# Sample states decayed ahead of their corrections, with four smaller moves in the queues, in a fused decoder layer

## The chip, the cores and the metric

The kernel runs on one core of one Trainium2 chip. The metric is the device time of one execution in microseconds (us), of which several runs are taken. The core has five engines with a queue of instructions each, which each engine works through in order: PE (TensorE, matmuls), ACT (ScalarE), DVE (VectorE), POOL (GpSimd) and SP (SyncE, which here issues most DMAs). POOL can issue DMAs as well. Instructions wait on semaphores for what other engines or DMAs have to have done.

## The reference

One layer of a hybrid decoder, for a prompt of 1024 tokens (x 1024 channels) and for 8 sample sequences of one token each, with shared weights, all in fp32. Cut to what matters:

```
h   = rmsnorm(x) * (1 + scale1) + shift1
qkv, gate, beta, a, sq, sk, sv, ga, gb = split(h @ w_in)
y_a = gated_rmsnorm(gated_delta_rule(conv4(qkv))) @ w_gdn_out     # 8 heads, 128 x 128 state each
y_b = sliding_window_attention(sq, sk, sv) @ w_swa_out
x   = x + gate1 * ((sigmoid(ga) * y_a + sigmoid(gb) * y_b) @ w_o)
h2  = rmsnorm(x) * (1 + scale2) + shift2
x   = x + gate2 * ((silu(conv3(h2 @ w_ffn_gate)) * (h2 @ w_ffn_up)) @ w_ffn_down)
y   = rmsnorm(x)
```

For a sample, the delta rule is one step on the state S of each head and sequence, which is an output too:

```
S     = S * exp(g)                                  # decay
delta = (v - k @ S) * beta
S     = S + outer(k, delta)                         # correction
o     = q @ S
```

## The kernel before

Matmuls of fp32 accuracy are made of three: each operand x is split into a high part (`wh`, `b1h`, ..., an ACT copy to a short format, L129) and a low part (`wl`, `b1l`, ..., a DVE subtraction, L130), and PE adds high x high (L180), high x low and low x high (L181, L182). `load_w` loads a weight tile of 1024 x 128 into `raw` (SP, L135) and splits it. In the stage of the two output projections w_swa_out and w_gdn_out there is one `raw` buffer, so that the load of the next tile is issued only when the low part of the one before has been made. Tokens come in blocks of 384, 384 and 264 columns, the last with the 8 samples.

The sample part is `sample_delta`, a generator whose pieces are woven among the matmuls of the output projections. The 64 sample states of 128 x 128 (8 heads x 8 sequences) lie in SBUF, three heads to a tile, in tiles named `b1h`, `b1l` and again `b1h`. 128 matmuls read them (L1172); copies (L1176) and a transpose bring the products k @ S and q @ S into columns; `delta` is computed in columns, transposed and written to DRAM as `dlr` (L1194). For each head SP loads its row of `dlr` spread over all 128 partitions (L1214, 512 KB written, into one of two rooms named `b1l`). Then ACT scales each 128 x 128 piece of it by k (L1216, 64 times), DVE makes S * egb + that piece in one instruction (L1217, 64 times; `egb` holds exp(g)), and POOL issues the store of the head's states (L1219). Between these, the root of the output's norm runs on POOL (`power`, L125), and its result leads to the sample columns (`osm`) of the operand of w_gdn_out.

Then comes w_o (`output_pass`, in four quarters q of the columns, 256 or 260 each), whose weights `output_weights(j)` loads (L1448) and splits. Its outputs x are squared and summed over channels for the second norm: ones-matmuls on PE (L1496), scale on DVE (`rs`, L1501), power -1/2 on POOL (L125), diagonal matrix on DVE (`dg`, L1505), spread by PE (L1506). The first FFN tile pair (`pair_weights`, `pair_product`) uses sums and differences of quarters of the operands and weights, a fast matrix product of seven terms: `ws` are weight sums on POOL (L1589), `minus` are differences of operands on DVE (L1538), `X` the operands, `pk` and `bmh`/`bml` some of their parts. The last norm, of q = 3, runs while the first FFN products of the left half have begun.

The order of each queue comes from the tile framework, which schedules by priorities. `weave` gives the pieces of several generators priorities from a start and a step, `later(f, by)` shifts those of one piece, and `issue_after(x)` holds the instructions within it behind instruction x in the planning.

Of the kernel before, what the change touches and what calls it, by code (L numbers as in the profile page):

```python
# [12 lines left out]
AF = mybir.ActivationFunctionType  # L13
ALU = mybir.AluOpType
# [4 lines left out]
P = 128  # L19
NP = 1024  # L20
NS = 8
NT = NP + NS
KC = 8
H = 8
# [40 lines left out]
class Step:  # L65
# [56 lines left out]

    def power(self, out, in_, expo):
        e = expo[:in_.shape[0], :]
        self.nc.gpsimd.tensor_tensor(out, in_, e.broadcast_to(list(in_.shape)), op=ALU.pow)  # L125

    def split(self, hi, lo, x, eng=None):

# [992 lines left out]
    def sample_delta(self, pool2):  # L1121

        nc, I = self.nc, self.I
        zl, cw = self.zl, self.cw
        S0, load = self.S0, self.load_state
        small = carver(*(self.flat_room(pool2, "b2", x, 2) for x in "hl"))
        act, tmp = small(24, NS), small(24, NS)
        nc.vector.tensor_tensor(act, zl[:, 3:11, :].rearrange("p b c -> p c b"), bc(cw[:, 3, :], 2, NS), op=ALU.mult)
        nc.vector.tensor_tensor(act, act, self.gsp, op=ALU.add)
        nc.scalar.activation(tmp, act, AF.Tanh, scale=0.5)  # L1130
        nc.vector.scalar_tensor_tensor(act, tmp, 1.0, act, op0=ALU.add, op1=ALU.mult)

        flat = lambda a: a.rearrange("p a h b -> p (a h b)")
        f3 = lambda a: a.rearrange("p h b -> p (h b)")
        qk = act[:, 0:16, :].rearrange("p (a h) b -> p a h b", a=2)
        v = act[:, 16:24, :]
        sq = small(2, H, NS)
        nc.vector.tensor_tensor(sq, qk, qk, op=ALU.mult)
        wide = small(H, NS, 2 * NS)
        nc.gpsimd.memset(wide, 0.0)  # L1140
        yield
        c, db = (self.flat_room(self.b1, "b1", x, 2) for x in "hl")
        load(6, c)
        load(7, c)
        ps = self.t(self.psm, [P, 1], "mm")
        nc.tensor.matmul(ps, flat(sq), self.ones[:, 0:1], start=True, stop=True)
        r = self.rows_rsqrt(small, ps, P, 1.0, 4 * EPS)
        yield
        rl = self.rows_spread(*r).rearrange("p (a h b) -> p a h b", a=2, h=H)
        kq = self.const([P, H, NS, 2], "kq")  # L1150
        nc.vector.tensor_tensor(kq[:, :, :, 0], qk[:, 1], rl[:, 1], op=ALU.mult)
        nc.vector.scalar_tensor_tensor(kq[:, :, :, 1], qk[:, 0], P ** -0.5, rl[:, 0], op0=ALU.mult, op1=ALU.mult)
        for i in range(2):
            nc.vector.tensor_copy(wide.rearrange("p h b c -> p h (b c)")[:, :, i::2 * NS + 2], kq[:, :, :, i])
        yield
        pr = small(H, NS)
        nc.vector.tensor_tensor(pr, kq[:, :, :, 0], kq[:, :, :, 1], op=ALU.mult)
        dots = self.t(self.psm, [P, H, NS], "mm")
        nc.tensor.matmul(f3(dots), self.ones, f3(pr), start=True, stop=True)
        qkd = small(H, NS)  # L1160
        nc.vector.tensor_copy(qkd, dots)
        yield
        eg = self.egb[:, :, 0, :].rearrange("p b h -> p h b")
        beta = self.egb[:, :, 1, :].rearrange("p b h -> p h b")

        rows = small(2, P, r=1)
        nc.gpsimd.memset(rows, 0.0)
        for i in range(2):
            ps = self.t(self.psm, [P, P], "mm")
            for b in range(NS):  # L1170
                for h in range(4):
                    nc.tensor.matmul(ps[32 * h:32 * h + 2 * NS], wide[:, 4 * i + h, b, :], S0[4 * i + h][:, b, :],  # L1172
                                     start=b == 0, stop=b == NS - 1)
            for h in range(4):
                at = slice(32 * h, 32 * h + 2 * NS)
                (nc.scalar.copy if h % 2 else nc.vector.tensor_copy)(rows[at, i, :], ps[at])  # L1176
            yield
        pks = self.t(self.psm, [P, 2 * P], "mm")
        for i in range(2):
            self.transpose(pks[:, i * P:(i + 1) * P], rows[:, i, :])  # L1180
        pks = pks.rearrange("p (h c) -> p h c", c=32)[:, :, :2 * NS].rearrange("p h (b a) -> p h b a", a=2)
        yield
        pk, dl, o = small(H, NS, 2), small(H, NS), small(H, NS)
        nc.vector.tensor_tensor(pk, pks, bc(eg, 3, 2), op=ALU.mult)
        nc.vector.tensor_scalar_mul(dl, v, 0.5)
        nc.vector.tensor_tensor(dl, dl, pk[:, :, :, 0], op=ALU.subtract)
        nc.vector.tensor_tensor(dl, dl, beta, op=ALU.mult)
        yield
        ps = self.t(self.psm, [H * NS, P], "mm")
        self.transpose(ps, f3(dl))  # L1190
        dlT = small(P, r=1)[:H * NS]
        nc.vector.tensor_copy(dlT, ps)
        dlr = self.t(self.dr, [H, NS, P], "dlr")
        nc.sync.dma_start(dlr.rearrange("h b v -> (h b) v"), dlT)  # L1194
        yield
        nc.vector.tensor_tensor(o, qkd, dl, op=ALU.mult)
        nc.vector.tensor_tensor(o, o, pk[:, :, :, 1], op=ALU.add)

        nc.vector.tensor_tensor(pr, o, o, op=ALU.mult)
        yield  # L1200
        ps = self.t(self.psm, [H * NS, 1], "mm")
        nc.tensor.matmul(ps, f3(pr), self.ones[:, 0:1], start=True, stop=True)
        r = self.rows_rsqrt(small, ps, H * NS, 1.0 / P, EPS)
        yield
        rl = self.rows_spread(*r).rearrange("p (h b) -> p h b", h=H)
        nc.vector.tensor_tensor(o, o, rl, op=ALU.mult)
        self.osm = self.const([P, H, NS], "osm")
        nc.vector.scalar_tensor_tensor(self.osm, o, self.onw, self.sgs, op0=ALU.mult, op1=ALU.mult)

        for h in range(H):  # L1210
            if h % 4 == 0:
                yield
            d = db[:, h % 2 * NP:h % 2 * NP + NP].rearrange("p (b v) -> p b v", b=NS)
            nc.sync.dma_start(d, dlr[h].unsqueeze(0).broadcast_to([P, NS, P]))  # L1214
            for b in range(NS):
                nc.scalar.activation(d[:, b, :], d[:, b, :], AF.Copy, scale=kq[:, h, b, 0:1])  # L1216
                nc.vector.scalar_tensor_tensor(S0[h][:, b, :], S0[h][:, b, :], self.egb[:, b, 0, h:h + 1], d[:, b, :],  # L1217
                                               op0=ALU.mult, op1=ALU.add)
            nc.gpsimd.dma_start(self.O[3][0][:, h].rearrange("b k v -> k b v"), S0[h])  # L1219

    def rows_rsqrt(self, small, ps, n, scale, eps):

# [180 lines left out]
    def room(self, tag, shape):  # L1403
        pool = self.bm if tag[0] == "b" else self.pk if int(tag[2]) < 4 else self.pk2
        return self.t(pool, shape, tag, F32R)

    def output_pass(self, pool, q):

        nc = self.nc
# [3 lines left out]
        def add(t, ps):  # L1413
            self.add_gated(t, ps, j, 16)
            sq = self.t(pool, [P, QW], "nsq" if j else "nss", bufs=2)[:, :n]
            if q == 3 and j > 4:
                nc.vector.tensor_tensor(sq, x1[:, j, :], x1[:, j, :], op=ALU.mult)
            else:
                nc.scalar.activation(sq, x1[:, j, :], AF.Square)
            if j == 0:  # L1420
# [5 lines left out]
                self.squares[q].append(sq)  # L1426

        for j in range(8):
            if q == 0:
                self.wo.append(self.output_weights(j))  # L1430
            nc.sync.dma_start(x1[:, j, :], self.xT[j][:, lo:lo + n])
            if q or j:
# [46 lines left out]
    def second_norm(self, pool, psum, t):  # L1479

        nc = self.nc
# [17 lines left out]
        for w, c0, c1 in ((P, 0, 2), (n - 2 * P, 2, nc_)):  # L1499
            if c0 < c1:  # L1500
                nc.vector.tensor_scalar(rs[:w, c0:c1], ss[:w, c0:c1], 1.0 / NP, EPS, op0=ALU.mult, op1=ALU.add)  # L1501
        self.power(rs[:, :nc_], rs[:, :nc_], self.mhalf)
        yield
        dg = self.t(pool, [P, 3, P], "dg", bufs=1)[:, :nc_]
        nc.vector.tensor_tensor(dg, bc(self.ident, 1, nc_), bc(rs[:, :nc_], 2, P), op=ALU.mult)  # L1505
# [15 lines left out]
    def operands(self, pool, p, stage):  # L1521
# [13 lines left out]
            yield  # L1535
            return
        d = self.t(pool, [P, 4, QW], "td", bufs=1)[:, :, :n]
        minus = lambda out, x, y: self.nc.vector.tensor_tensor(out, x, y, op=ALU.subtract)  # L1538
        minus(a1, b1, a1)
        self.split(*ops[3], a1)  # L1540
        yield
        minus(d, b2, a1)
        self.split(*ops[2], d)
        yield
        minus(b1, b2, b1)
        self.split(*ops[4], b1)
        yield
        minus(a2, a2, d)
# [104 lines left out]
    def ffn_gate_up(self, pool, pool2, psum, f, w, first):  # L1653
# [36 lines left out]

        if first:
            ss, r = self.norm_at
            self.pair_product(psum, w, (0,), gate, {2: ss, 4: r})
        self.pair_product(psum, w, (1,) if first else (0, 1), gate)
        w = self.pair_weights(pool, I["w_ffn_up"][0], f, nc.vector if first else None)

        def up(p, i, q, ps, r):
# [206 lines left out]
    def second_half(self):  # L1904

        nc, S = self.nc, ExitStack
        with S() as c:
# [6 lines left out]
            with S() as right:  # L1914
                xr = self.pool("xr", 1, ctx=right, side="right")
                with S() as left:
                    xl = self.pool("xl", 1, ctx=left)
                    self.x1 = [self.t(pl, [P, KC, n], "x1") for pl, (_, n) in zip((xl, xr), HALF)]
                    self.x1d = self.t(self.dr, [KC, P, NT], "x1d")
                    self.squares, self.X, self.wo = {}, {}, []  # L1920
                    norm = lambda q: self.second_norm(xr, psum, q)
                    self.weave((chain(*(self.output_pass(xr, q) for q in range(4))), 0, 1),
                               (self.ffn_states(xr, psum), 460, 30),
# [2 lines left out]
                               (chain(norm(2), self.operands(xr, 1, 0)), 730, 120))  # L1926
                with S() as left:
                    pool = self.pool("pf", 1, ctx=left)
                    w = self.pair_weights(pool, self.I["w_ffn_gate"][0], 0)
                    last, ops = norm(3), self.operands(xr, 1, 1)  # L1930
                    self.weave((chain(islice(last, 3), islice(ops, 1), last, ops), -100, 1))
                    right.close()
# [139 lines left out]
```

## Time and profile before

| what | value |
|---|---|
| median of 3 runs | 2085.34 us |
| lowest and highest | 2084.30 and 2087.26 us |
| profiled execution, span of its instructions | 2084.4 us |
| mean granted TensorE clock in it | 0.991 |
| PE busy | 2012.7 us, 97% |
| DVE, ACT, POOL busy | 65%, 43%, 25% |

The page gives the profiled execution as its span, with no second time; the median of the runs stands 0.9 us above that span. A row of the trace gives a start in us from the span's beginning, a length in us, the engine, the line, what is written and read, and in brackets for how long the engine stood idle before it and what ended that. A view of windows gives for each stretch its length, the busy time of PE, PE's weight loads, DVE, ACT and POOL with the number of instructions, the granted clock, the DMA share and GB/s.

### The profile page before, as it was taken

Reading aid. Unit: us, or ns where it says so; the run is one execution under the profiler, and the core shown is the slowest. Engines: PE = TensorE matmul, PEld = TensorE weight load, DVE = VectorE, ACT = ScalarE, POOL = GpSimd, SP = SyncE. Lnnn points to the kernel's source line nnn. Section 1 sums busy time; section 2 is a strip of 40 time slices with the busy share of each in tenths; the row PEclk is TensorE's granted clock in tenths of the full one; section 3 lists DMA queues with packets and bytes.
Section 4 is the critical chain, followed back from the end, with each engine's and each line's share of the span. In section 5 each row is a group of like instructions: output and inputs, shape, how many; then the busy total and the mean of one; then the engine's idle time right before and its main releaser. Section 6 shows DMA issues by size and latency. Waiting matters only on the chain.

```text
span 2084.4 us, 41297 instructions
## 1 busy us (share of the span) xinstructions
PE 2012.7 (97%) x16245; PEld 1910.2 (92%) x16245; DVE 1347.8 (65%) x2714; ACT 900.2 (43%) x2233; POOL 520.2 (25%) x594
## 2 busy tenths in 40 slices
PE   7999998999999999989989999999999999999897
PEld 4987877799999999989989999999999999999897
DVE  5755768473655647656544675578876776767756
ACT  4664545433344243432342542354444444534443
POOL 2000000121321221201111000005575466446421
PEclk9999999999999999999999999999999999999999
DMA  8256443331332322312275855323333333488862
GB/s 300 62 144 210 135 167 116 117 94 51 80 80 61 73 72 52 89 42 62 63 223 172 285 186 163 112 63 97 105 91 112 102 92 112 136 305 266 291 215 94
DMA packets 301887, 275.75 MB, mean 132 GB/s; under 512 B 59730, under 2 KB 248111, under 8 KB 301676
## 3 DMA queue, kind: packets, MB, share of 16 engines
q1 hardware_dynamic: 295642, 252.14, 39.6%
q0 software_dynamic: 5552, 20.37, 2.8%
q8 instruction: 127, 2.08, 0.4%
q14 instruction: 68, 0.56, 0.1%
q10 hardware_dynamic: 498, 0.61, 0.1%
HBM read 212.93 MB, written 62.51 MB: 132 GB/s over the span
## 4 chain that ended last, share of the span: by engine, by line
PE 83%; DVE 5%; DMA 5%; ACT 3%; issue 1%; SPq 1%; POOL 1%; DVEq 0%; POOLq 0%; ACTq 0%
PE mm L180 19%; PE mm L181 18%; PE mm L182 18%; PE wv L180 3%; PE wv L182 3%; PE wv L181 3%; PE wy L182 2%; PE wy L180 2%; PE wy L181 2%; PE pv L652 1%; PE pt L190 1%; PE tp L190 1%; DVE x L1472 1%; PE mm L264 1%; PE rc L954 1%
## 5 line engine op out<-in xcount | busy, mean ns | idle before, releaser
L180 PE MATMUL mm<-b1h,wh 128*128 128x384 f32 (+1 forms) x1520 | 496.9, 328 | 3.7 <-ACT gt L1294 1.6
L181 PE MATMUL mm<-b1l,wh 128*128 128x384 f32 (+1 forms) x1520 | 489.3, 323 | 0.0
L182 PE MATMUL mm<-b1h,wl 128*128 128x384 f32 (+1 forms) x1520 | 488.0, 323 | 0.3 <-DVE wl L130 0.3
L180 PEld LDWEIGHTS mm<-b1h,wh 128*128 128x128 f32 x1520 | 286.7, 189 | 12.4 <-issue 4.6
L181 PEld LDWEIGHTS mm<-b1l,wh 128*128 128x128 f32 x1520 | 287.1, 189 | 4.4 <-issue 3.1
L182 PEld LDWEIGHTS mm<-b1h,wl 128*128 128x128 f32 x1520 | 286.3, 189 | 3.9 <-issue 2.8
L129 ACT ACTIVATE wh<-raw 128x1024 fp32r<-128x1024 f32 x83 | 87.0, 1049 | 122.4 <-PE mm L181 70.2
L130 DVE TENSOR_TENSOR wl<-raw,wh 128x1024 fp32r<-128x1024 f32 x82 | 101.0, 1233 | 57.2 <-ACT wh L129 55.1
L181 PE MATMUL mm<-pk,w 128*128 128x260 f32 (+1 forms) x440 | 124.8, 284 | 1.1 <-DVE pk L130 1.1
L180 PE MATMUL mm<-pk,w 128*128 128x260 f32 (+1 forms) x440 | 124.8, 284 | 0.0
L182 PE MATMUL mm<-pk,w 128*128 128x260 f32 (+1 forms) x440 | 124.5, 283 | 0.0
L130 DVE TENSOR_TENSOR w<-ws,w 128x512 fp32r<-128x512 f32 x88 | 78.0, 886 | 36.9 <-ACT w L129 36.7
L1626 ACT COPY bml<-mm 128x256 f32<-128x256 f32 (+1 forms) x132 | 48.9, 371 | 100.6 <-PE mm L182 96.7
L180 PE MATMUL mm<-bmh,w 128*128 128x260 f32 (+1 forms) x320 | 90.3, 282 | 0.0
L182 PE MATMUL mm<-bmh,w 128*128 128x260 f32 (+1 forms) x320 | 90.1, 282 | 0.0
L1681 DVE SCALAR_TENSOR_TENSOR fa<-fz,fcw,fa 128x512 f32<-128x512 f32 x88 | 75.2, 874 | 18.2 <-ACT fa L1679 17.9
L180 PE MATMUL mm<-b2h,wh 128*128 128x384 f32 (+1 forms) x256 | 83.2, 328 | 2.9 <-ACT wh L129 2.8
L181 PEld LDWEIGHTS mm<-pk,w 128*128 128x128 f32 x440 | 83.2, 189 | 1.3 <-DVE pk L130 1.3
L181 PE MATMUL mm<-b2l,wh 128*128 128x384 f32 (+1 forms) x256 | 83.6, 327 | 0.4 <-DVE b2l L130 0.4
L180 PEld LDWEIGHTS mm<-pk,w 128*128 128x128 f32 x440 | 83.2, 189 | 0.2 <-ACT bml L1626 0.2
L182 PEld LDWEIGHTS mm<-pk,w 128*128 128x128 f32 x440 | 83.4, 190 | 0.0
L182 PE MATMUL mm<-b2h,wl 128*128 128x384 f32 (+1 forms) x256 | 82.8, 326 | 0.0
(645 smaller groups left out, 5886.2 us busy)
## 6 DMA issues: line engine op xcount, KB each, us to landing
raw<-in_w_in_dram SPq DMA_DIRECT2D x59, 512.0 KB
ws<-in_w_ffn_down_dram SPq DMA_DIRECT2D x55, 256.0 KB
raw<-xd SPq DMA_DIRECT2D x47, 258.0 KB
raw<-in_w_ffn_down_dram SPq DMA_DIRECT2D x47, 256.0 KB
raw<-in_w_ffn_gate_dram SPq DMA_DIRECT2D x22, 512.0 KB
raw<-in_w_ffn_up_dram SPq DMA_DIRECT2D x22, 512.0 KB
qst<-in_w_mod_dram SPq DMA_DIRECT2D x16, 512.0 KB
raw<-in_w_mod_dram SPq DMA_DIRECT2D x16, 512.0 KB
```

Source lines behind the costliest of these rows:

```text
L129: self.nc.scalar.activation(hi, x, AF.Copy)
L130: (eng or self.nc.vector).tensor_tensor(lo, x, hi.bitcast(F32), op=ALU.subtract)
L180: mm(ps, whi, xhi, start=first, stop=False, **kw)
L181: mm(ps, whi, xlo, start=False, stop=False, **kw)
L182: self.last_mm = mm(ps, wlo, xhi, start=False, stop=last, **kw).ins
L190: self.nc.tensor.transpose(out, in_, self.ident[:p, :p])
L264: nc.tensor.matmul(ps[32 * j:32 * j + 32], self.cT[:, k0 + j, :], ws[j // 2][:, j % 2, :], start=k0 == 0, stop=k0 > 0)
L652: nc.tensor.matmul(pv[64 * r:64 * r + 64], V[:, n - back, ch], ps[:, r::2, :], start=back == 0, stop=back == (n > 0))
L954: yield step(nc.tensor.matmul(ds, kd[:, n, :], s, start=True, stop=True))
L1472: nc.vector.scalar_tensor_tensor(x[:, :np_], ps[:, :np_], by[:, j, 8:9], x[:, :np_], op0=ALU.mult, op1=ALU.add)
L1626: self.last_copy = nc.scalar.copy(r[p, i], x[p])
L1681: nc.vector.scalar_tensor_tensor(ai[:, c:e], zi[:, j + c:j + e], col(j), ai[:, c:e], op0=ALU.mult, op1=ALU.add)
```

## The change

1. `decay_states` multiplies the 64 states by `egb` in place, on ACT (L1236), in pieces from the matmuls that read them on. The scaling of the spread rows on ACT is gone: DVE's instruction is now d * k + S (L1225). The spread rows go by POOL's queue (L1216 of the changed kernel), two at the start and each later one behind the store (L1227) of the head two before.
2. `output_weights` for j < 3 is called ahead of the weaving with `later(..., -150)`, no longer in `output_pass`.
3. The first root of the second norm goes on record (`first_root`), and the weights of the first FFN tile are held behind it.
4. The first product of the left half (pair 0) is held behind the last square (`last_square`), and the first products of pair 1 behind the last norm's sums (`ss`).
5. In pair 1 the difference `minus(b1, b2, b1)` goes to POOL.

```diff
+        decay = self.decay_states()
+        next(decay)
         pks = self.t(self.psm, [P, 2 * P], "mm")
 ...
-        yield
+        next(decay)
+        yield
+        next(decay)
         pk, dl, o = small(H, NS, 2), small(H, NS), small(H, NS)
 ...
         yield
+        next(decay)
         ps = self.t(self.psm, [H * NS, P], "mm")
 ...
+        room = lambda h: db[:, h % 2 * NP:h % 2 * NP + NP].rearrange("p (b v) -> p b v", b=NS)
+        spread = lambda h: nc.gpsimd.dma_start(room(h), dlr[h].unsqueeze(0).broadcast_to([P, NS, P]))
+        yield
+        spread(0)
+        spread(1)
         for h in range(H):
-            if h % 4 == 0:
+            if h == 4:
                 yield
-            d = db[:, h % 2 * NP:h % 2 * NP + NP].rearrange("p (b v) -> p b v", b=NS)
-            nc.sync.dma_start(d, dlr[h].unsqueeze(0).broadcast_to([P, NS, P]))
+            d = room(h)
             for b in range(NS):
-                nc.scalar.activation(d[:, b, :], d[:, b, :], AF.Copy, scale=kq[:, h, b, 0:1])
-                nc.vector.scalar_tensor_tensor(S0[h][:, b, :], S0[h][:, b, :], self.egb[:, b, 0, h:h + 1], d[:, b, :],
+                nc.vector.scalar_tensor_tensor(S0[h][:, b, :], d[:, b, :], kq[:, h, b, 0:1], S0[h][:, b, :],
                                                op0=ALU.mult, op1=ALU.add)
             nc.gpsimd.dma_start(self.O[3][0][:, h].rearrange("b k v -> k b v"), S0[h])
+            if h + 2 < H:
+                spread(h + 2)
+
+    def decay_states(self):
+
+        for h in range(H):
+            for b in range(NS):
+                s = self.S0[h][:, b, :]
+                self.nc.scalar.activation(s, s, AF.Copy, scale=self.egb[:, b, 0, h:h + 1])
+            if h % 2:
+                yield
 ...
-            if q == 0:
+            if q == 0 and j > 2:
                 self.wo.append(self.output_weights(j))
 ...
-        self.power(rs[:, :nc_], rs[:, :nc_], self.mhalf)
+        root = self.power(rs[:, :nc_], rs[:, :nc_], self.mhalf)
+        if t == 0:
+            self.first_root = root
 ...
-        minus(b1, b2, b1)
+        minus(b1, b2, b1, self.nc.gpsimd if p else self.nc.vector)
 ...
-            self.pair_product(psum, w, (0,), gate, {2: ss, 4: r})
-        self.pair_product(psum, w, (1,) if first else (0, 1), gate)
+            with self.tc.issue_after(self.last_square.ins):
+                self.pair_product(psum, w, (0,), gate, {2: ss, 4: r})
+        self.pair_product(psum, w, (1,) if first else (0, 1), gate, {0: ss, 1: ss} if first else {})
 ...
+                    for j in range(3):
+                        self.wo.append(self.later(lambda: self.output_weights(j), -150))
 ...
-                    w = self.pair_weights(pool, self.I["w_ffn_gate"][0], 0)
+                    with self.tc.issue_after(self.first_root.ins):
+                        w = self.pair_weights(pool, self.I["w_ffn_gate"][0], 0)
```

On ACT, in the stage of w_swa_out, before (`wh` are high parts of weight tiles; the row of `wh_12807` begins at 1139.33 in the trace, that of `wh_12982` at 1153.48 and that of `wh_13019` at 1159.58):

```order
L129 ACTIVATE wh_12807<-raw_12805 128x1024
L1176 COPY b2l_2048_12698<-mm_12850 16x128 x2
L129 ACTIVATE wh_12845<-raw_12843 128x1024
L1176 COPY b2l_2048_12698<-mm_12915 16x128 x2
L129 ACTIVATE wh_12982<-raw_12980 128x1024
L1106 COPY z_13039<-mm_13040 96x256
L1107 COPY z_13039<-mm_13040 72x128
L129 ACTIVATE wh_13019<-raw_13017 128x1024
```

The same place now; twenty more rows L1236 stand between `wh_12807` and the first one shown:

```order
L1176 COPY b2l_2048_12698<-mm_12850 16x128
L1236 ACTIVATE b1h_1875_11803<-b1h_1875_11803,egb 128x128 x5
L129 ACTIVATE wh_12845<-raw_12843 128x1024
L1236 ACTIVATE b1h_1875_11803<-b1h_1875_11803,egb 128x128 x3
L1236 ACTIVATE b1l_1876_11804<-b1l_1876_11804,egb 128x128 x5
L1176 COPY b2l_2048_12698<-mm_12850 16x128
L1236 ACTIVATE b1l_1876_11804<-b1l_1876_11804,egb 128x128 x5
L1176 COPY b2l_2048_12698<-mm_12915 16x128
L1236 ACTIVATE b1l_1876_11804<-b1l_1876_11804,egb 128x128 x10
L1236 ACTIVATE b1h_2051_12733<-b1h_2051_12733,egb 128x128 x2
L129 ACTIVATE wh_12982<-raw_12980 128x1024
```

So 50 decays, three copies and one other split now stand between the splits `wh_12807` and `wh_12982`; the other 14 stand between `wh_12982` and the next split.

On POOL, at the start of the FFN, before (`rs` are the roots of the second norm by quarters, `ws` the weight sums of the first FFN tile):

```order
L1393 DMA sgx_14296<-sga_2614 128x264
L1589 TENSOR_TENSOR ws_15523<-raw_15513,raw_15515 128x512
L1589 TENSOR_TENSOR ws_15525<-ws_15523,raw_15513 128x512
L1589 TENSOR_TENSOR ws_15533<-raw_15513 128x512
L125 TENSOR_TENSOR rs_15396<-rs_15396,mhalf 128x2
L125 TENSOR_TENSOR rs_15431<-rs_15431,mhalf 128x2
```

and now:

```order
L1412 DMA sgx_14296<-sga_2614 128x264
L125 TENSOR_TENSOR rs_15396<-rs_15396,mhalf 128x2
L1610 TENSOR_TENSOR ws_15523<-raw_15513,raw_15515 128x512
L1610 TENSOR_TENSOR ws_15525<-ws_15523,raw_15513 128x512
L1610 TENSOR_TENSOR ws_15533<-raw_15513 128x512
L125 TENSOR_TENSOR rs_15431<-rs_15431,mhalf 128x2
```

The first root has moved ahead of the three weight sums. On ACT around the first split of w_o (`w_14338`, high part) the rows before are

```order
L129 ACTIVATE bmh_2117_13460<-t_2040_12684 128x4
L129 ACTIVATE bmh_2119_13462<-t_2040_12684 128x260
L129 ACTIVATE w_2200_14338<-raw_14336 128x512 x2
L129 ACTIVATE pk_2205_14376<-raw_14374 128x1024
L129 ACTIVATE w_2209_14412<-raw_14410 128x1024
```

and now

```order
L129 ACTIVATE bmh_2117_13460<-t_2040_12684 128x4
L129 ACTIVATE bmh_2119_13462<-t_2040_12684 128x260
L129 ACTIVATE w_2200_14338<-raw_14336 128x512 x2
L129 ACTIVATE pk_2203_14346<-raw_14344 128x1024
L129 ACTIVATE w_2205_14351<-raw_14349 128x1024
```

Only numbers of tiles differ.

More of the change, by code (lines that the diff above doesn't have):

```diff
@@ L124, in power @@
         e = expo[:in_.shape[0], :]
-        self.nc.gpsimd.tensor_tensor(out, in_, e.broadcast_to(list(in_.shape)), op=ALU.pow)
+        return self.nc.gpsimd.tensor_tensor(out, in_, e.broadcast_to(list(in_.shape)), op=ALU.pow)
     def split(self, hi, lo, x, eng=None):
@@ L1416, in add @@
             if q == 3 and j > 4:
[L1417 removed]
+                self.last_square = nc.vector.tensor_tensor(sq, x1[:, j, :], x1[:, j, :], op=ALU.mult)
             else:
@@ L1537, in operands @@
         d = self.t(pool, [P, 4, QW], "td", bufs=1)[:, :, :n]
-        minus = lambda out, x, y: self.nc.vector.tensor_tensor(out, x, y, op=ALU.subtract)
+        minus = lambda out, x, y, eng=self.nc.vector: eng.tensor_tensor(out, x, y, op=ALU.subtract)
         minus(a1, b1, a1)
```

## The prediction

> **What bounds the kernel now.** I read the page first (span, busy shares, chain of waits), then PE's waits in the stretch in which the change moves instructions, then the granted clock there, then the queues one by one.
>
> ```profile
> span 2084.4 us, 41297 instructions
> ...
> PE 2012.7 (97%) x16245; PEld 1910.2 (92%) x16245; DVE 1347.8 (65%) x2714; ACT 900.2 (43%) x2233; POOL 520.2 (25%) x594
> ...
> PE 83%; DVE 5%; DMA 5%; ACT 3%; issue 1%; SPq 1%; POOL 1%; DVEq 0%; POOLq 0%; ACTq 0%
> ```
>
> PE is busy for 97% of the span and carries 83% of the chain. The change takes no matmul away, so it can only gain or lose where PE stands still, or runs at half clock. PE's waits from 1140 to 1430 us, the whole stretch that the change touches (for what, total, times, longest):
>
> ```profile
> PE mm L180 <- ACT wh L129: 2.8, 1, 2.8
> PE mm L1439 <- ACT w L129: 2.1, 1, 2.1
> PE nr L1506 <- DVE dg L1505: 1.6, 1, 1.6
> PE wv L180 <- ACT w L129: 1.1, 1, 1.1
> PE mm L181 <- DVE pk L130: 1.1, 1, 1.1
> PE mm L182 <- DVE pk L130: 0.8, 1, 0.8
> PE wv L181 <- DVE pk L130: 0.3, 1, 0.3
> ```
>
> I call them A (2.8, a w_gdn_out tile at 1192), B (2.1, the first w_o tile at 1282), E (0.8, at 1302), D (1.6, the first root of the second norm, at 1321) and C (0.3, 1.1 and 1.1 at 1405 to 1410, the last norm's operands). That is 9.8 us in all, less than 0.5% of the span. The clock adds to it. Where I cut the trace into pieces of 3.41 us (PE busy is the second figure, the granted clock stands behind POOL's):
>
> ```profile
> 888.30:891.71 3.41, 1.64 (x68) 1.31 (x68) 3.30 (x4) 0.37 (x1) 0.00 (x0) 1.00 0.51 149
> 1086.28:1089.69 3.41, 1.67 (x10) 1.28 (x10) 2.48 (x3) 2.21 (x3) 0.00 (x0) 1.00 0.72 238
> 1192.09:1195.50 3.41, 0.58 (x4) 0.48 (x4) 3.08 (x10) 3.41 (x9) 0.53 (x1) 1.00 1.05 390
> 1195.50:1198.91 3.41, 3.41 (x17) 3.41 (x16) 3.41 (x6) 2.29 (x4) 0.35 (x1) 0.50 1.06 400
> 1280.84:1284.25 3.41, 1.60 (x14) 1.39 (x12) 1.82 (x6) 1.03 (x4) 0.00 (x0) 1.00 0.21 46
> 1407.13:1410.54 3.41, 1.22 (x8) 0.81 (x7) 3.41 (x5) 1.44 (x2) 0.00 (x0) 1.00 0.00 0
> 1410.54:1413.95 3.41, 3.41 (x18) 3.41 (x17) 3.12 (x5) 1.21 (x3) 0.00 (x0) 0.50 0.76 258
> ```
>
> The pieces at 1195.50 and 1410.54 run at 0.50, each just behind a piece in which PE worked for less than half (0.58 and 1.22 of 3.41). At half clock 3.41 us do the work of 1.71, so each costs 1.7 us: A and C cost 4.5 and 4.2 us, not 2.8 and 2.5. The piece of B had 1.60 busy and kept its clock; those at 888.30 and 1086.28 had 1.64 and 1.67 and stand ahead of the other two drops of this half of the trace. So about half of a piece is the edge, and B lies on it.
>
> The Trainium skill ("TensorE: Matmul & The Clock Gate", "Why this matters for your kernels") asks for no idle gap of PE above about 3 us. C's longest wait is 1.1 us and the clock fell, so the trace is stricter than the page; by the page no stall here, old or new, should touch the clock, which is the third rival below.
>
> **The change, part by part. The decays.** The 64 scalings of the correction rows leave ACT's queue at 1177 to 1194, and 64 decays of the states enter it from the matmuls that read the states, at 1140.43, on. In the new order 50 of them, three copies and a weight split stand ahead of the split that began at 1153.48. What is there now, on ACT, then SP, then PE:
>
> ```profile
> 1153.48 1.06 ACT L129 ACTIVATE wh<-raw 128x1024 fp32r<-128x1024 f32 x1 [2.97 <-DMA raw<-in_w_swa_out_dram]
> ...
> 1159.58 1.06 ACT L129 ACTIVATE wh<-raw 128x1024 fp32r<-128x1024 f32 x1 [1.34 <-DMA raw<-in_w_swa_out_dram]
> ...
> 1168.12 1.06 ACT L129 ACTIVATE wh<-raw 128x1024 fp32r<-128x1024 f32 x1 [2.69 <-DMA raw<-in_w_swa_out_dram]
> 1174.85 1.06 ACT L129 ACTIVATE wh<-raw 128x1024 fp32r<-128x1024 f32 x1 [5.66 <-DMA raw<-in_w_swa_out_dram]
> 1177.67 4.80 ACT L1216 ACTIVATE b1l<-b1l,kq 128x128 f32<-128x128 f32 x16 [1.77 <-DMA b1l<-dlr]
> ...
> 1183.04 1.05 ACT L129 ACTIVATE wh<-raw 128x1024 fp32r<-128x1024 f32 x1
> ...
> 1191.58 2.45 ACT L1216 ACTIVATE b1l<-b1l,kq 128x128 f32<-128x128 f32 x8 [2.36 <-DMA b1l<-dlr]
> 1193.93 1.04 ACT L129 ACTIVATE wh<-raw 128x1024 fp32r<-128x1024 f32 x1
> ```
>
> ```profile
> 1155.82 0.38 SPq L135 DMA_DIRECT2D raw<-in_w_swa_out_dram  x1
> ...
> 1161.92 0.40 SPq L135 DMA_DIRECT2D raw<-in_w_swa_out_dram  x1
> ...
> 1170.47 0.38 SPq L135 DMA_DIRECT2D raw<-in_w_swa_out_dram  x1
> ...
> 1177.19 0.38 SPq L135 DMA_DIRECT2D raw<-in_w_gdn_out_dram  x1
> ...
> 1185.60 0.38 SPq L135 DMA_DIRECT2D raw<-in_w_gdn_out_dram  x1
> ```
>
> ```profile
> 1140.43 0.30 PE L1172 MATMUL mm<-b1h,b2h 128*16 128x128 f32 x3
> ...
> 1157.42 0.42 PE L180 MATMUL mm<-b2h,wh 128*128 128x384 f32 x1
> ...
> 1161.69 0.42 PE L180 MATMUL mm<-b1h,wh 128*128 128x384 f32 x1
> ...
> 1195.02 0.45 PE L180 MATMUL mm<-b2h,wh 128*128 128x384 f32 x1 [2.83 <-ACT wh L129]
> ```
>
> One scaling takes 4.80/16 = 0.30 us, and a decay is the same operation on the same 128x128. So 50 x 0.30 = 15.0, one split 1.06 and three copies of some 0.2 (estimate: less than a scaling, on 16 rows) make 16.7 us from 1140.5: the split of 1153.48 begins at 1157.2 and ends at 1158.3. PE wants that tile at 1157.42 now, and some 0.4 earlier in the new order, which puts transposes behind it. **New stall: 1.3 us**, and 0.3 more for its low half (the DVE part behind the split).  If the decays start at 1142 instead, when the last of the first matmuls are done, it is 2.8.
>
> The load buffer is single: the next load goes out only when the low half is done, which takes some 1.3 us after the split (issues at 1155.82 and 1161.92 stand 1.28 behind the splits' ends at 1154.54 and 1160.64). So the load of 1155.82 goes out at 1159.6. From issue to split these loads took 3.76, 6.20 and 4.38 us (1155.82 to 1159.58, 1161.92 to 1168.12, 1170.47 to 1174.85). I take the row's own 3.76 and the next short one's 4.38, mean 4.1: split from 1163.7 to 1164.8. PE, now 1.6 late, wants it at 1161.69 + 1.6 = 1163.3: **1.5 us more**, and 0.4 for the low half. With 6.20 it would be 3.6. In sum the decays cost **3.7 us** (2.5 to 6).
>
> Behind that, **A**. Before, the split of 1193.93 stood behind 8 scalings that waited 2.36 us for a row spread, and the one of 1183.04 behind 16 scalings, though its load (issued 1177.19) would, at 4.1, have been there at 1181.3. Both covers go. The chain of loads is 4.1 us late where PE is 3.7 late, and saves 1.75 at 1183.04: the last load goes out at 1185.60 + 4.1 - 1.75 = 1188.0. It took up to 8.33 (1185.60 to 1193.93, of which the scalings hide the end); I take 7.5, near that end, as DMA engines stay as busy. Split done at 1196.5; PE, which stopped at 1192.2, wants it at 1195.9: 0.6 is left of 2.83, a **gain of 2.2** (1.4 to 2.8).
>
> What hides the rest: DVE does the 64 updates as before. The row spreads move from SP to POOL, which has 25% of its time in use; the root of the output norm stands behind two of them there, and what it delays, the sample columns of w_gdn_out's operands, is first wanted with the tile split at 1183.04; later than that it would stop the whole stage. DVE's first update now waits for a spread at the head of its queue, ahead of the evacuations L1341 and the low halves: free as long as the spread is there when DVE comes, up to 3 us (another A) if it takes over 7 us.
>
> **w_o's first loads and splits ahead by 150.** On SP, ACT and DVE these rows stand in the same order as before. B stays: 0.
>
> **First root.** POOL did it behind three sums of weights that waited for their load:
>
> ```profile
> 1317.59 1.28 POOL L1589 TENSOR_TENSOR ws<-raw,raw 128x512 f32<-128x512 f32 x1 [38.91 <-DMA raw<-in_w_ffn_gate_dram]
> ...
> 1321.43 0.73 POOL L125 TENSOR_TENSOR rs<-rs,mhalf 128x2 f32<-128x2 f32 x1
> ```
>
> ```profile
> 1315.19 0.16 DVE L1501 TENSOR_SCALAR rs<-nr 128x2 f32<-128x2 f32 x1 [2.43 <-PE nr L1496]
> ...
> 1322.19 0.43 DVE L1505 TENSOR_TENSOR dg<-ident,rs 128x256 f32<-128x256 f32 x1 [4.72 <-POOL rs L125]
> ```
>
> Now it goes first: root at 1315.4 + 0.73, dg 0.43 later with some 0.1 between, at 1316.7. PE's L1506 stood 49 rows behind the last sum, which ended about 1315.0, and PE got there at 1321.0 (1322.62, when dg was done, less the wait of 1.6): 0.12 us a row. Now it stands 34 rows behind, at 1319.1. D goes: **-1.6 us**. The three sums start no later than their load, at 1317.59.
>
> **Last norm's sums** go up 15 rows on PE, and of the four differences of 128x1040 one goes from DVE to POOL:
>
> ```profile
> 1403.38 1.24 DVE L1538 TENSOR_TENSOR x<-x 128x1040 f32<-128x1040 f32 x1
> ```
>
> DVE gets to the splits behind it 1.24 earlier, which ends two of C's three waits (0.3 and 1.1 <- DVE pk); the third is for ACT, whose queue is no shorter, and inherits what is late next. POOL needs two times and a bit the 1.28 of 512 columns, 2.6 us, and its result is split last but one, some 4 us later. I take **-0.7 us** (0 to -1.3).
>
> **Clock.** A's piece and C's should keep theirs: 0.6 and 1.8 us of stall, the latter in two places, leave more than half: -3.4. But the new stalls, 1.6 and 1.9 within 7 us, and B lie at the edge; I count one new drop among the three: +1.7. **Net -1.7** (-3.4 to +1.7).
>
> **Sum**: 3.7 - 2.2 - 1.6 - 0.7 - 1.7 = -2.5 us. The profiled span, 2084.4, lies 0.9 below the median of the three runs (2085.34) and at the lowest (2084.30), so next to nothing lies around it and I take the difference to the median: **2082.8 us**. What a measurement of this kernel can tell from no change is some 0.2%, 4.2 us.
>
> **The rivals.** First, no new drop of the clock: -2.5 - 1.7 = -4.2, and with the decays at their low end of 2.5 and A's gain at 2.8 it would be -6.0. I put it between, at -4.9: 2080.4. For it: neither new stall alone fills half a piece. Against: they add up if a piece boundary falls well for them.
>
> Second, on the other side, the single load buffer. With every load of this stretch at 6.2, as that of 1161.92 took, the second stall is 3.6 instead of 1.5 and the load of A goes out 2 us later and is 2.6 late instead of 0.6; both pieces then drop and so does the first: +3.7 + 2.1 + 2.0 - 2.2 - 1.6 - 0.7 + (3 - 2) x 1.7 = +5.0, 2090.3. It decides from a mean of about 6 us. For it: in A's piece the DMA share was 1.05, and the load there did take over 6. Against: two of three loads took 4.4 or less.
>
> Third, the half-clock pieces do not follow the stalls, and none goes or comes: -0.8, 2084.5. Against it stand the four rows. It is what the page's rule would give, since no wait here comes to 3 us.
>
> **How the numbers follow.** Forecast (2081.2 to 2085) 0.43, first rival 0.34, second 0.14, third 0.09. Faster by over 0.2% is the first rival alone, 0.34; slower the second, 0.14; the rest 0.52. The range goes from -6.5, the first rival with the best ends of the decays, A and C, to +2.7, about half way to the second: 2078.8 to 2088.
>
> **What would show it.** In the changed profile: PE waits on ACT wh L129 of 1.3 and 1.5 us at 1157 and 1164, where now are none; none above 1 us at 1195; no wait on dg before L1527; the wait of 2.1 before the w_o matmul unchanged; one wait of 1 to 1.4 us at 1405 to 1412. The forecast is wrong if the first two are missing (decays shorter or later placed by what they wait for), if the spreads hold DVE, or if more than one piece behind them runs at 0.50.

## The result and the profile after

The changed kernel is slower by 0.3%: 2091.23 us median (2087.35 to 2093.44, 17 runs) beside 2085.01 us for the kernel before (2079.26 to 2093.31, 17 runs), a ratio of 1.0029 with a 95% interval of 1.0021 to 1.0036, or +6.2 us. The profiled execution had a span of 2086.9 us at a mean clock of 0.989 and a time of 2088.84 us; so some 1.9 us lie around a span, where the prediction had taken next to nothing.

PE's waits of the changed kernel in the stretch that the prediction walked through, 1130 to 1440 us (for what, total, times, longest):

```profile
PE mm L180 <- ACT wh L129: 5.5, 3, 3.2
PE mm L1458 <- ACT w L129: 2.1, 1, 2.1
PE mm L181 <- DVE pk L130: 1.8, 1, 1.8
PE wv L181 <- DVE pk L130: 1.1, 1, 1.1
PE mm L182 <- DVE pk L130: 0.8, 1, 0.8
```

The wait on `dg` (D) is gone, B's 2.1 and E's 0.8 are as before. Weight splits are waited for three times instead of once, the longest time still 3.2 us, and the two waits on DVE `pk` (C) have grown from 0.3 and 1.1 to 1.1 and 1.8, while C's third (1.1 on ACT `w`) is gone. The granted clock, by pieces of 3.41 us as in the prediction:

```profile
1197.41:1200.83 3.42, 0.66 (x4) 0.33 (x2) 0.73 (x2) 0.68 (x1) 1.45 (x2) 1.00 1.08 363
1200.83:1204.24 3.41, 2.99 (x12) 2.99 (x13) 3.00 (x9) 2.58 (x4) 0.00 (x0) 0.50 1.06 409
1412.45:1415.87 3.42, 1.66 (x14) 1.45 (x14) 3.42 (x5) 1.59 (x2) 0.00 (x0) 1.00 0.00 0
1415.87:1419.28 3.41, 3.37 (x17) 3.08 (x16) 3.41 (x6) 1.50 (x3) 0.00 (x0) 0.50 0.83 303
```

Both half-clock pieces are still there, each again behind a piece in which PE worked for less than half (0.66 and 1.66). ACT's and SP's rows where the decays stand and where A stood:

```profile
1156.17 3.04 ACT L1236 ACTIVATE b1l<-b1l,egb 128x128 f32<-128x128 f32 x10
1159.11 0.68 ACT L1236 ACTIVATE b1h<-b1h,egb 128x128 f32<-128x128 f32 x2
1159.69 1.04 ACT L129 ACTIVATE wh<-raw 128x1024 fp32r<-128x1024 f32 x1
...
1165.87 1.06 ACT L129 ACTIVATE wh<-raw 128x1024 fp32r<-128x1024 f32 x1
...
1200.15 1.06 ACT L129 ACTIVATE wh<-raw 128x1024 fp32r<-128x1024 f32 x1 [6.87 <-DMA raw<-in_w_gdn_out_dram]
```

```profile
1162.02 0.38 SPq L135 DMA_DIRECT2D raw<-in_w_swa_out_dram  x1
...
1190.73 0.37 SPq L135 DMA_DIRECT2D raw<-in_w_gdn_out_dram  x1
```

The decays run without a break up to the split at 1159.69. The sum had 1157.2, and this execution already ran 2.0 us behind the one of before at 1140, so the split is some 0.5 later than reckoned. At A no scaling stands ahead of the split any more: ACT was idle for 6.87 us there and the load itself took 9.42 us, from 1190.73 to 1200.15.

To see where the time went without what differs by chance elsewhere, I took the start of the same-numbered PE matmul in each trace and looked at how far a kernel falls behind the first profile of before from mark to mark. The marks are at 1140, 1180, 1250, 1300, 1340 and 1440 us of that profile; the last column is their sum.

| kernel | decays 1140-1180 | A 1180-1250 | B 1250-1300 | E, D 1300-1340 | C 1340-1440 | sum |
|---|---|---|---|---|---|---|
| before, second profile | 0.0 | -0.4 | +1.5 | +1.4 | -0.1 | +2.3 |
| changed | +3.9 | +0.2 | 0.0 | -1.9 | +1.4 | +3.5 |
| changed, second profile | +5.3 | -0.1 | +1.5 | -2.6 | +1.4 | +5.4 |
| decays_only | +3.8 | +1.3 | +0.2 | -0.8 | -0.1 | +4.4 |
| decays_sp_rows | +5.3 | -3.2 | +1.5 | -2.3 | -0.4 | +0.8 |
| small_moves | 0.0 | -0.6 | -0.1 | -2.6 | +1.3 | -1.9 |
| root_only | 0.0 | +0.2 | -0.1 | -1.8 | -0.4 | -2.0 |
| root_sums | 0.0 | -0.6 | +0.7 | -1.7 | -0.5 | -2.2 |
| after_dve_minus | +3.9 | -0.7 | +1.4 | -3.3 | +0.1 | +1.4 |
| thin_rows | +3.8 | -3.7 | +0.8 | -2.3 | +1.6 | +0.2 |
| thin_stores | +3.7 | -2.6 | -0.1 | -2.4 | +0.1 | -1.1 |
| spaced | +0.6 | +6.2 | 0.0 | -2.1 | +0.1 | +4.7 |
| spaced_low | +0.2 | +2.2 | -0.1 | -1.8 | +0.1 | +0.7 |

### The profile page after: what moved, and what is told of

Same layout as the page of the kernel before. It is cut to its first block, busy times and chain, and to the rows that moved or that the text cites. A ratio compares the mean times of both kernels' runs of the same rounds, so it can differ in the third digit from the quotient of the medians.

```text
span 2086.9 us, 41282 instructions
## 1 busy us (share of the span) xinstructions
PE 2016.1 (97%) x16245; PEld 1911.3 (92%) x16245; DVE 1354.1 (65%) x2713; ACT 901.0 (43%) x2233; POOL 526.1 (25%) x603
## 4 chain that ended last, share of the span: by engine, by line
PE 81%; DMA 7%; DVE 5%; ACT 3%; issue 1%; SPq 1%; POOL 1%; DVEq 0%; POOLq 0%; ACTq 0%
PE mm L180 18%; PE mm L181 18%; PE mm L182 18%; PE wv L180 2%; PE wv L182 2%; PE wv L181 2%; PE wy L180 1%; PE wy L182 1%; PE wy L181 1%; PE pv L652 1%; DMA ws<-in_w_ffn_down_dram 1%; PE pt L190 1%; PE tp L190 1%; DMA raw<-in_w_ffn_down_dram 1%; PE mm L264 1%
```

## The experiments

Theory 1 was: the decays cost what stands ahead of the weight splits (+3.9), A stays because it is a slow load and not ACT's scalings, the root gains 2.0, and POOL's difference costs more in the last norm than it saves. The rivals were that the loss sits in one part alone, or that A was luck of one run.

**One part alone.** Four kernels of one set; before took 2087.59 us in it (35 runs).

```diff
# decays_only: before with sample_delta and decay_states of the changed kernel
# small_moves: changed kernel with sample_delta of before
# root_only: before with
+        root = self.power(rs[:, :nc_], rs[:, :nc_], self.mhalf)
+        if t == 0: self.first_root = root
+        with self.tc.issue_after(self.first_root.ins): w = self.pair_weights(...)
# after_dve_minus: changed kernel with
-        minus(b1, b2, b1, self.nc.gpsimd if p else self.nc.vector)
+        minus(b1, b2, b1)
```

> The kernel before with the sample part of the changed kernel alone (early decays on ACT, rows by POOL's queue). Theory 1, terms as in the changed kernel's profile: PE waits on ACT wh of 1.7 + 0.9 and some 0.4 us on the low halves at 1158 to 1168 (+3.9 us), the wait at 1195 to 1200 for the w_gdn_out tile stays at 2.8 to 3.5 (0), so +4 us against before. Rival, the decays cost nothing on balance and the loss sits in the last norm: 0 us (within 1.5).

Measured: 2092.54 us, ratio 1.0016 (1.0003 to 1.0030), so +3.3 us. PE's waits on weight splits in its whole stretch:

```profile
PE mm L180 <- ACT wh L129: 6.4, 3, 4.1
```

Two of the three, 2.3 us in sum, lie at 1150 to 1180, the third, 4.1, is A. The decays lose time where they stand and take nothing off A; the rival falls.

> The changed kernel with the sample part of before: w_o's first loads, first root, last norm's sums and the difference on POOL remain. Theory 1: -2.0 (wait on dg gone) + 1.4 (last norm) = -0.6 us against before. Rival, the loss sits in the last norm: +4 us or more.

Measured: 2085.59 us, ratio 0.9994 (0.9984 to 1.0004), -1.3 us: theory 1. The last norm costs 1.3 in the table, far from 4.

> Before with the first root ahead of the weight sums on POOL, alone. Theory 1: the PE wait on DVE dg of 1.6 us at 1321 goes and nothing takes its place: -1.8 us. Rival, hidden or paid back in the first FFN tile, whose weight sums start later: 0.

Measured: 2085.51 us, ratio 0.9986 (0.9977 to 0.9996), -2.9 us. POOL's root runs at once and the weight sums begin when their load lands:

```profile
1321.09 0.73 POOL L125 TENSOR_TENSOR rs<-rs,mhalf 128x2 f32<-128x2 f32 x1 [36.93 <-DVE rs L1501]
1322.95 1.29 POOL L1591 TENSOR_TENSOR ws<-raw,raw 128x512 f32<-128x512 f32 x1 [1.13 <-DMA raw<-in_w_ffn_gate_dram]
```

PE has no wait on `dg` left, and nothing is paid back later (-1.8 at the root, -2.0 over the whole stretch). The column of the root is noisy by itself: kernels that leave the root where it was have +1.4, -0.8 and -2.3 in it. The wait is the firmer sign: it is in all four profiles with the root in its old place (0.8 to 2.4 us) and in none of the ten with the root moved. By time this version is 0.14% under before; the other kernels with the root moved and without the decays, small_moves and root_sums, can't be told from before.

> The changed kernel with the difference b2 - b1 back on DVE. Theory 1: the DVE split of 128x1040 beside POOL's difference takes 1.24 again instead of 3.42 us, DVE does 1.24 more, PE's two waits on DVE pk at 1410 to 1415 shrink by about 1 us in sum: 1 us under the changed kernel, +5 against before. Rival, no contention and the split was late for another reason: PE's waits grow by 1.2 us, +7.5 against before.

Measured: 2087.91 us, ratio 1.0005 (0.9993 to 1.0017), +1.0 us against before where the changed kernel had +6.2 in its own set. Expected was +5, so by the times this one line is worth some 5 us and not 1 (the two intervals, 0.9993 to 1.0017 and 1.0021 to 1.0036, do not meet); the traces explain only a part of that. The changed kernel's rows, DVE then POOL:

```profile
1407.22 1.24 DVE L1559 TENSOR_TENSOR td<-x 128x1040 f32<-128x1040 f32 x1 [0.30 <-ACT x L1538]
1408.45 3.42 DVE L130 TENSOR_TENSOR pk<-x,pk 128x1040 fp32r<-128x1040 f32 x1
```

```profile
1407.26 3.51 POOL L1559 TENSOR_TENSOR x<-x 128x1040 f32<-128x1040 f32 x1 [9.92 <-ACT x L1538]
```

and DVE's with the difference back on it, which stands second and the split third:

```profile
1402.48 1.24 DVE L1559 TENSOR_TENSOR td<-x 128x1040 f32<-128x1040 f32 x1 [0.30 <-ACT x L1538]
1403.64 1.24 DVE L1559 TENSOR_TENSOR x<-x 128x1040 f32<-128x1040 f32 x1
1404.80 1.23 DVE L130 TENSOR_TENSOR pk<-x,pk 128x1040 fp32r<-128x1040 f32 x1
```

From the start of the difference into `td` to the split's end DVE took 4.65 us beside POOL (1407.22 to 1411.87) and 3.55 us without it (1402.48 to 1406.03). The help cost 1.1 us on DVE. The rival, no contention, falls.

**The last norm by parts.** root_sums is before with the root and the sums moved, so it differs from small_moves in POOL's difference and in the calls of w_o's weights.

> Before with the first root and the last norm's sums moved, nothing else. Theory 1: -2.0 for the root; the last norm without POOL's difference about -0.5: -2.5 us against before. Rival, the sums' move by itself is what costs in the last norm: +1.4 - 2.0 = -0.6.

Measured: 2083.20 us beside 2085.82 us of before, but a ratio of only 0.9996 (0.9983 to 1.0009), -0.8 us; by time it can't be told from before. In the table column C is -0.5 with the sums alone, +0.1 with the calls of w_o's weights besides (after_dve_minus) and +1.3 with the difference on POOL too (small_moves). So the line on POOL costs some 1.2 us, and the calls 0.6. The 0.6 is lost between the marks 1360 and 1380, in small_moves and in all kernels made from the changed one, and in none made from before. There the calls have changed PE's order: sums of an earlier quarter of the second norm, which stand together in root_sums,

```profile
1365.04 0.59 PE L1496 MATMUL nr<-ones,nsq 128*128 128x1 f32 x4
1365.56 0.19 PE L1496 MATMUL nr<-ones,nss 128*4 128x1 f32 x2
1365.61 0.24 PE L1496 MATMUL nr<-ones,nsq 128*4 128x1 f32 x4
```

stand one by one between FFN products in after_dve_minus:

```profile
1364.64 0.19 PE L1515 MATMUL nr<-ones,nss 128*4 128x1 f32 x2
1364.76 0.39 PE L182 MATMUL mm<-bmh,pk 128*128 128x260 f32 x1
1365.08 0.19 PE L1515 MATMUL nr<-ones,nsq 128*4 128x1 f32 x2
1365.20 0.39 PE L180 MATMUL mm<-bmh,pk 128*128 128x260 f32 x1
1365.51 0.19 PE L1515 MATMUL nr<-ones,nsq 128*4 128x1 f32 x2
```

The half-clock piece behind C goes with the order of the last norm as well. All three profiles with the difference on POOL (two of the changed kernel, small_moves) have the piece behind C, and none of the six with the sums moved and the difference on DVE has it. Of the five with the sums in their old place three have it and two (root_only, decays_sp_rows) do not. It is worth little here: these two have -0.4 in column C where the other three have 0.0 or -0.1, because without the piece PE is 1.4 us ahead up to 1430 and gives 1.0 back at another wait, 0.7 us for `bml` at 1437 in root_only.

**What A is.** Bytes are taken away beside the slow load, so that the states that come out are incomplete; both start from after_dve_minus.

```diff
# thin_rows, from the third head on
-                spread(h + 2)
+                spread(h + 2, 16)          # 16 of 128 partitions
# thin_stores, for all heads but the last
-            nc.gpsimd.dma_start(self.O[3][0][:, h].rearrange("b k v -> k b v"), S0[h])
+            nc.gpsimd.dma_start(self.O[3][0][:, h].rearrange("b k v -> k b v")[:m], S0[h][:m])   # m = 16
```

> As the kernel with the difference back on DVE, but from the third head on the row spread writes 16 partitions instead of 128, so these corrections are not computed rightly; all else is kept. It takes 6 x 448 KB of writes out of 1188 to 1215. Theory, the w_gdn_out load of 1186 is slow (9.7 us from issue to split) for the transfers beside it: it takes 6 to 8 us, PE's wait of 2.1 at 1196 falls under 1 and its half-clock piece goes, -2 to -4 us. Rival, the load is slow whatever is beside it, or waits for its queue: no change.

> As the kernel with the difference back on DVE, but of the first seven heads' states only 16 of 128 partitions are stored. It takes 7 x 448 KB out of 1185 to 1215. Same theories: the w_gdn_out load takes 6 to 8 us instead of 9.7 and PE's wait falls under 1 us, -2 to -4 us; or no change. If rows matter and stores do not, or the reverse, it is not the bytes alone.

Measured: thin_rows 2087.87 us, ratio 1.0010 (0.9996 to 1.0023); thin_stores 2086.25 us, 0.9999 (0.9986 to 1.0012). The times alone tell neither from after_dve_minus. The stretch of A does: -3.7 and -2.6 where after_dve_minus had -0.7. The loads took 7.0 and 8.1 us from issue to split instead of 9.7, and PE's longest wait for a split there, which was 2.1, is in thin_rows

```profile
PE mm L180 <- ACT wh L129: 0.7, 1, 0.7
```

and in thin_stores

```profile
PE mm L180 <- ACT wh L129: 0.8, 1, 0.8
```

No half-clock piece follows in either. So A is a load made slow by the transfers beside it, whichever they are. In all profiles of kernels of before's order the same load took 7.8 to 8.8 us, in those with the rows on POOL's queue and nothing thinned 9.3 to 11.3.

> Before with the early decays alone, but the rows' spreads issued by SP as before. Theory 1: the new waits at 1158 to 1168 stay (+3.9); the w_gdn_out load takes 8 to 9 us from issue to split as in before, not 9.4 to 10.2, so that +3.5 us or less remain of the +4.4 of the decays with POOL's queue. Rival, the queue that issues the rows does not matter: +4.4.

```diff
-        spread = lambda h: nc.gpsimd.dma_start(room(h), ...)
+        spread = lambda h: nc.sync.dma_start(room(h), ...)       # in decays_only
```

Measured: 2091.11 us beside 2086.21 us, ratio 1.0031 (1.0018 to 1.0044). In the table A falls by 3.2 us; the load takes 8.5 us, PE's wait is 1.1 us and no half-clock piece follows. The changed kernel's second profile, which like this one lost 5.3 us at the decays, has -0.1 at A with a load of 9.7. So the queue of the rows does matter to A, as far as one profile shows it. Yet the time is no better than that of decays_only. In this profile a half-clock piece stands behind the new stalls and one behind B, and 4.6 us were lost ahead of the stretch; five runs don't settle what the queue is worth.

The Trainium skill ("DMA: Bandwidth & Descriptors", "Queues, rings and completion order") says that each DMA engine takes turns between the queues it has work for. From 1185 to 1205 us POOL's queue took 37.0% of the DMA engines' time in the changed kernel and 19.4% in this one, where the rows stand in the load's own queue instead. The durations of the load go with the share of POOL's queue; no run here shows the turns themselves.

**Decays that stand ahead of no split.** From after_dve_minus, the decays in four lots of 16, three of them behind a weight split each:

```diff
+                with self.tc.issue_after(self.his[n - 2 + h // 2 - 1].ins) if h > 1 else nullcontext():
                     self.nc.scalar.activation(s, s, AF.Copy, scale=self.egb[:, b, 0, h:h + 1])
# spaced_low, besides: the updates behind the low half of the last w_swa_out tile
+                with self.tc.issue_after(self.w_lo.ins):
                     nc.vector.scalar_tensor_tensor(S0[h][:, b, :], d[:, b, :], ...)
```

> As the kernel with the difference back on DVE, but the decays of heads 2 to 7 queued in three lots of 16 behind a weight split each, so that no more than 16 decays (4.9 us) stand between two splits of w_swa_out tiles. Theory 1, the decays cost by standing ahead of the splits: the PE waits of 1.7 and 0.9 us and the late low halves at 1158 to 1168 go, -3.9 us against that kernel; the wait for the w_gdn_out tile stays at 2 to 4. Rival, the cost is in the rows' new queue or in the decays wherever they stand: 0.

Measured: 2094.42 us, ratio 1.0036 (1.0022 to 1.0049). The new stalls are gone, as theory 1 said: no PE wait at all from 1150 to 1180 us. But 6.2 us are lost behind, on one wait:

```profile
PE mm L181 <- ACT wh L129: 6.4, 1, 6.4
```

DVE's and SP's rows ahead of it:

```profile
1183.54 2.19 DVE L1226 SCALAR_TENSOR_TENSOR b1h<-b1l,kq,b1h 128x128 f32<-128x128 f32 x8 [2.22 <-DMA b1l<-dlr]
1185.65 0.56 DVE L1363 TENSOR_TENSOR t<-mm,gt 128x384 f32<-128x384 f32 x1
1186.11 1.22 DVE L130 TENSOR_TENSOR wl<-raw,wh 128x1024 fp32r<-128x1024 f32 x1
```

```profile
1177.61 8.94 SPq L1415 DMA_DIRECT2D gt<-sgb  x2
1186.71 2.51 SPq L1272 DMA_DIRECT2D b2l<-oa  x4
1189.33 0.49 SPq L136 DMA_DIRECT2D raw<-in_w_gdn_out_dram  x1
```

DVE stood before its first update until the row came at 1183.5; the evacuation and the low half behind it came late, and with them the gate load that waits for the evacuation's buffer and all that SP has behind it. The load of the next tile went out at 1189.33, 7.8 us behind the start of the split before it, where after_dve_minus took 2.3 from the one to the other (1176.54 to 1178.88).

> As the kernel with spaced decays, but DVE's updates of the states queued behind the low half of the last w_swa_out tile, so that they cannot stand ahead of it while they wait for the first row. Theory: the wait of 6.4 us at 1195 came from that low half being 3.5 us late and shrinks to 2 to 4, with one half-clock piece in place of three: -5 to -7 us against the spaced kernel. Rival, it came from SP's queue, where the load stands behind two gate loads and the operand's loads: 0 to -2 us.

Measured: 2088.04 us, ratio 1.0009 (1.0000 to 1.0018), 6.4 us under spaced by the medians and 5.6 by the ratios, in two sets. The waits there fall to

```profile
PE mm L183 <- DVE b2l L130: 2.5, 2, 1.9
PE mm L182 <- ACT b2h L129: 1.6, 1, 1.6
```

with one half-clock piece in place of three. The updates at the head of DVE's queue were the larger part of that stall. Spaced and queued so, the decays cost next to nothing where they stand, and A still takes 2.2 us more than in before: even then there is no gain in them.

**Both kernels once more.**

> The changed kernel once more, for a second profile. Theory 1, the terms of the first profile are the kernel's own: waits of 1.7 and 0.9 at 1158 to 1168, some 3 us and a half-clock piece at 1195 to 1200, none on dg, the split of 128x1040 near 3.4 us beside POOL's difference; +3.5 to +6 us against before. Rival, the w_gdn_out wait and the half-clock piece behind it are luck of one run: one of them missing, less than +3.

> The kernel before once more, for a second profile: the stretch from 1135 to 1440 us takes as long as in the first profile within 1 us by theory 1; by the rival the w_gdn_out wait or a half-clock piece is missing and it is 2 to 4 us shorter, which would carry the part of the loss that the first two profiles do not show.

Measured: the changed kernel 2091.56 us beside 2086.21 us, ratio 1.0030 (1.0018 to 1.0041); one run of before at 2087.19 us. A and the piece behind it are in all four profiles (waits of 2.8, 2.4, 3.2 and 2.7 us); the rival falls. The second profile of before did not keep to what was expected of it: its stretch took 2.3 us longer than the first one's, not the same within 1. A piece behind B comes and goes with the run. In before's second profile:

```profile
1280.46:1283.88 3.42, 1.45 (x12) 1.23 (x11) 1.89 (x5) 1.04 (x5) 0.00 (x0) 1.00 0.23 62
1283.88:1287.29 3.41, 3.32 (x15) 3.33 (x16) 3.22 (x6) 2.46 (x4) 0.00 (x0) 0.50 0.75 215
```

B's wait of 2.1 us is the same, only the boundary fell otherwise: 1.45 us busy, where it was 1.60, and 1.5 us are lost behind. The other 1.4 us lie in the next column, where the wait on `dg` was 2.4 us instead of 1.6 and a half-clock piece follows it.

## Why the prediction was wrong

**The decays: right.** +3.7 forecast (its parts, 1.3, 0.3, 1.5 and 0.4, add to 3.5, which would make the whole sum -2.7), +3.9 and +5.3 in the two profiles (with a half-clock piece in the second). The waits for the two splits were 1.6 and 0.7 us in the first profile, at the places named: the split of `wh_12982` stood behind 50 decays, and the single load buffer carried the delay to the next tile. `spaced` shows it, where both stalls vanish with the 50 in a row.

**A: the step that failed first.** I credited 2.2 us to A. The two profiles have +0.2 and -0.1. The wait was put down to ACT because the split stood right behind 8 scalings, but the load under it took up to 8.3 us, and without the scalings it is plainly the load that is waited for. Taking the scalings away did not shorten the time from its issue to its split: 8.5 us in decays_sp_rows, where the rows stay in SP's queue, beside 7.8 to 8.8 in before's order. My own sum held 7.5 us for that load; it took 9.4 (and 9.7 and 10.2 in the kernels with the same rows). With 9.4 in the sum, 2.5 of the 2.83 us remain. So the term was mis-sized on a duration that I took at the low side of the only row I had. The rows' move to POOL's queue, which I had weighed for POOL's work and not for the load, made it longer still: with the rows left to SP, A did fall by 3.2 us in the one profile there is.

**C: the second.** I took -0.7, with POOL's 2.6 us as free. The profiles have +1.4. POOL took 3.51 and DVE's split beside it 3.42 instead of 1.24. I had the price of POOL by itself and no price of the two beside each other. The line on POOL makes some +1.2 of the +1.4, the sums' own move -0.5, and 0.6 comes from w_o's calls (below).

**Clock: the third, and it follows from those two.** -1.7 forecast, no change found: A's and C's pieces stay because A's and C's waits do. C's could not have given its 1.7 in any case, since the profiles without it gain only 0.3 to 0.4 in column C. A piece of 3.41 us with less than half of PE's work is followed by one at half clock in the rows shown above (0.66, 1.45 and 1.66 busy), but the prediction's 1.60 kept its clock, and half is no firm edge on the other side either. In the changed kernel's second profile, behind the decays, 1.86 was followed by a drop, and in thin_rows so was a full piece:

```profile
1161.91:1165.33 3.42, 1.86 (x9) 1.32 (x10) 2.39 (x5) 3.37 (x10) 0.00 (x0) 1.00 0.22 58
1165.33:1168.74 3.41, 3.41 (x12) 3.41 (x12) 0.77 (x4) 3.38 (x12) 0.00 (x0) 0.50 0.85 240
1365.15:1368.57 3.42, 3.42 (x31) 2.97 (x29) 1.91 (x5) 1.57 (x3) 0.00 (x0) 1.00 0.12 7
1368.57:1371.98 3.41, 3.41 (x18) 3.38 (x18) 0.77 (x3) 0.00 (x0) 0.86 (x1) 0.50 0.55 186
```

The latter makes thin_rows' +1.6 in column C, and what caused it stays open. So the pieces follow the stalls as a rule, not always. The third rival, by which they would not, has most rows against it, with waits that came to 3.2 us at A but only 2.1 at B and 1.8 at C. That B lies at the edge fits its 1.5 us in some profiles and not in others.

**D: right** (-1.6 forecast, -1.8 in root_only). **w_o: half right.** B stayed at 2.1 us, but I had compared the rows of SP, ACT and DVE and not those of PE, whose order the calls changed; the term taken as 0 was some +0.6.

With the terms as measured in the first profile (the 0.6 lies within the 1.4) the sum is 3.9 + 0.2 - 1.9 + 1.4 = +3.6 us, against -2.5 forecast; the signs of A, C and the clock make the difference. The second rival had the sign but not the way: it wanted every load at 6.2, while the load of 1162.02 took 3.85 to its split, and behind it only the one at A was much slower than in before.

Something stays open. The traces place 3.5 and 5.4 us in the changed stretch, and the second profile of before alone lost 2.3 there by chance, so the pairs differ by some 3.3 us, while the two sets of runs say 6.2 and 5.4. Outside the stretch the profiles lie between -2 and +7 us from each other ahead of it and up to 3.5 us behind it, with the same instructions, mostly by half-clock pieces that come and go. I can't say whether any of the remaining 2 to 3 us belongs to the change. It may go with the line on POOL: without it, in after_dve_minus, time (+1.0) and table (+1.4) agree. No run shows how.

## What to carry to other kernels

A wait that the profile puts down to the instruction which came last may hide a transfer that came just before it: look at when the load under it was issued and landed, and price the removal by the load, not by the instruction. A transfer that is moved to another queue is not free because the engine that issues it has time: look at the loads that run beside it. Work moved early into an engine's idle time costs what it stands ahead of: lay the tightest consumer's need beside the whole length of the lot, and break the lot at each such consumer. A single-buffered load chain carries each delay on to the next load.

## What was not expected of the hardware

DVE and POOL hardly worked beside each other on these operands. POOL's difference began at 1407.26, 0.04 us behind a DVE difference that ran its usual 1.24 us, and took 3.51; DVE's split began at 1408.45, took 3.42 and ended 1.10 us behind POOL's end at 1410.77. These rows look as if the three had run one after another: 1.24, then 2.3 of POOL, then 1.1. The second profile (3.51 and 3.42) and small_moves (3.50 and 3.41) have the same figures. The Trainium skill ("GPSIMD Engine Reference", "Specifications") says that POOL's ways to SBUF are shared with VectorE and that they contend when a DVE instruction has two SBUF inputs, as these have. The trace agrees and gives it a size, 2.2 us on a split of 1.24; I had not weighed it.
